# A hybrid four-layer network on one core: six edits to its order and its small operations

## The chip, the cores and the metric

The kernel runs on one core of one Trainium2 chip. The core has a matrix engine (TensorE, PE in the profile, with its weight loads shown as PEld), a vector engine (VectorE, DVE), an activation engine (ScalarE, ACT), GpSimd (POOL) and a queue engine for transfers (SyncE, SP). The time is the device time of one launch in microseconds (us); a kernel's time is the median of several runs. One more execution of the kernel was recorded by the hardware profiler; all rows below are from it.

## The reference

A sequence of 256 rows of 1024 numbers passes through two blocks of two layers each, all in float32. The projection weights are read from memory once; nothing is reused between layers.

```
def first_block(x, mem, ...):                 # the first two layers
    for l in range(DEPTH):
        mix = hybrid_mixer(h, ...)            # rnn branch + windowed attention with sinks
        h = layer_norm(ALPHA * h + mix, ...)                      # ln1
        h = layer_norm(ALPHA * h + cross_attention(h, mem, ...))  # ln2
        h = layer_norm(ALPHA * h + swiglu(h, ...))                # ln3
def rglru_branch(...):  # log_a = -8 * r * softplus(-lru_lambda), a scan over the sequence
def swa_sink_branch(...):
    probs = softmax(concatenate([scores, sink], axis=-1))[..., :-1]
def second_block(x, ...):                     # the last two layers
    for l in range(DEPTH):
        proj = rms_norm(x, pre_norm[l]) @ w_in[l]
        o = diff_attention(q, k, v, lam, rel_bias)   # w = p0 - lam * p1, then w @ v
        y_a = rms_norm(o) * (1 - lam_init) * silu(z_a)
        filt = hyena_filters(...)                    # depends on the weights alone
        z = fft_long_conv(hv, filt[:, 0]) * hx1
        z = fft_long_conv(z, filt[:, 1]) * hx2
        m = sigmoid(g_a) * (y_a @ w_pa[l]) + sigmoid(g_h) * (y_h @ w_ph[l])
        x = x + rms_norm(m @ w_out[l], post_norm[l])
```

## The kernel before

**Matrices.** Each float32 factor is split into a high part (suffix h) and a low part (suffix l), and a product takes three matmuls: high by high, high by low, low by high. A weight is loaded by SP into a tile `raw`, copied by ACT into `wh` (L240) and subtracted by DVE into `wl` (L242), in halves of 128x1024. Activations are turned by PE with transposes (L393) into a layout with features on partitions; the two parts are then taken from PSUM by ACT and DVE (`split`, L369 and L371). `fm` is a result with features on partitions, `tm` one with rows on partitions.

**Order.** PE and SP run in exactly the order in which the program issues their work. The orders on ACT, DVE and POOL are made by a scheduler at build time from priorities and an estimate of readiness. What the program issues is set by generators: one main stream walks over the weights, piece by piece, and beside it chains (`rnn_co`, the attentions, the filters) take turns. A chain hands over with `yield L["name"]`; the number in the table L (L46 to L53) says after how much estimated time it may go on. A larger number puts the next step of the chain, its PE instructions included, behind more matmuls of the main stream.

**The places of this change.** `vec_co` transposes the small vectors and computes the decay rates of the rnn branch on DVE and ACT (L580 to L592). `swa_run` does the windowed attention: scores from PSUM (L710), maximum (L714), maximum with the sink (L716), its negation (L717), exponentials (L721), transposes `pt`, row sums turned with `rb` (L746 reads them). `to_fm_block` transposes a normed block (`tx`), ahead of it a few matmuls on constants (`warm`, L529) whose count stands in `WARM`. The filters' last products `fh` are taken from PSUM by ACT into `ft` (L1354). `pre_co` does the norm ahead of the second block's projections. In `diff_attention` the weights `dsc` of two heads are transposed (`dw`), multiplied with v (`o`), normed (`yo`), transposed (`yt`) and split into `ya2h` and `ya2l`, which the next weight stream (`fm` from `ya2h`) reads. `c` is the last product of the inverse Fourier transform, from `Yh` and `Yl`.

Of the kernel before, what the change touches and what calls it, by code (L numbers as in the profile page):

```python
# [13 lines left out]
F32 = mybir.dt.float32  # L14
# [6 lines left out]
P = 128  # L21
# [25 lines left out]
    vec=6000, flt=12000, fh=1200, fe=18000, prep=15000, mlp=7500, sc=11000, rnn=7000, rnn2=11700,  # L47
    pt=3000, tx=0, spec=6000, sp0=3000, sp1=5000, sp2=5000, sp3=5000, ds=9000, dn=8960, do=5500,
    z=12000, cn=1000, cp=2000, ln_0=500, ln01=5500, ln02=5500, ln03=6800, ln_03=2300, ln11=6000, ln12=4000, pre0=5100,
    pre1=5000, rope=5000, sw0=1120, sw_end=1500, sw1=1000, sw2=1500, cv0=800, cv1=1050, rnn3=1800,  # L50
    rnn_end=3000, cx0=1500, cx1=1000, cx2=800, cx_end=1500, ml=7200, fm=3000, fm1=7500, fe0=4000, eo0=6000,
    eo1=12000, eo2=8000, fd=6000, di0=1500, dw=2300, di_end=1500, c30=770, c31=1300, hy0=1300,
    hy1=2000, hy2=500, hy3=1600, hy_end=2000, pre_n=3000, pre_b=2500, pre_n0=1000, pre_n1=2300, prep2=30000, mem=10200, mt=2500, vt=2500, vt2=12000)  # L53

# [35 lines left out]

WARM = {"ln0": 3, "ln1": 3, "pre0": (9, 0), "pre1": (9, 0), "pt": 4}

# [18 lines left out]
class Net:  # L111
    def __init__(self, ctx, tc, a):
        self.tc, self.nc, self.a = tc, tc.nc, a
        self.const = ctx.enter_context(tc.tile_pool(name="const", bufs=1))
        self.wraw = ctx.enter_context(tc.tile_pool(name="wraw", bufs=NRAW))
        self.wspl = ctx.enter_context(tc.tile_pool(name="wspl", bufs=NW))
        self.slots = ctx.enter_context(tc.tile_pool(name="slots", bufs=NSLOT))
        self.sm = ctx.enter_context(tc.tile_pool(name="sm", bufs=2))
        self.ps = ctx.enter_context(tc.tile_pool(name="ps", bufs=4, space=PSUM))
        self.pa = ctx.enter_context(tc.tile_pool(name="pa", bufs=4, space=PSUM))  # L120
        self.dr = ctx.enter_context(tc.tile_pool(name="dr", bufs=1, space=bass.MemoryType.DRAM))
        self.n = 0
        self.first_hi = None
        self.wm = None
        self.block_1 = None
        self.start = True

        self.pause, self.defer = False, None
        self.t = 0.0
        self.chains, self.bg, self.fill = [], [], True  # L130
        nc = self.nc
        self.ident = self.const.tile([P, P], F32, name="ident")
        make_identity(nc, self.ident)
        self.mhalf = self.const.tile([P, 4], F32, name="mhalf")
        nc.vector.memset(self.mhalf, -0.5)
# [356 lines left out]

    def to_fm_block(self, src, x, tb, warm=0, after=None):

        t = slice(tb * P, (tb + 1) * P)
        for q in range(2):
            ps = self.pch([4, P], "tx")
            self.busy(ps, 0 if q else warm)
            for i in range(4):
                k = q * 4 + i  # L500
                self.tr(ps[:, i, :], src[tb][:, k * P:(k + 1) * P])
            self.fm_ins = self.split(x[0][q][:, :, t], x[1][q][:, :, t], ps, after)
            if self.pause and tb == TB - 1 and q == 1:
                self.resume(self.fm_ins[1])
            yield L["tx"]
# [28 lines left out]
    def load_common(self):  # L534
# [4 lines left out]
        for nme in self.VEC1:  # L539
            if nme == "conv_w":  # L540
                cnt, s = 32, a[nme].rearrange("l k (c p) -> (k c) l p", p=P)
            else:
# [10 lines left out]
        nc.gpsimd.dma_start(self.sink, a["sinks"].rearrange("l h -> (l h)")[None, :]  # L553
                            .to_broadcast([P, DEPTH * 16]))

    def vec_co(self):
# [3 lines left out]
        for l in range(DEPTH):  # L560
# [9 lines left out]
            self.half_ig.append(hb)  # L570
            self.rates.append(self.decay_rates(l))
        if self.both:
            yield L["vt2"]
            yield from self.block2_vecs()

# [57 lines left out]
    def ln_co(self, l, i, t, hT):  # L633
# [5 lines left out]
        yield L[f"ln{l}{i}"] - first  # L639
        yield from self.to_fm_block(t, hT, 1, warm=WARM["ln1"] * self.pause)  # L640

# [45 lines left out]
    def swa_run(self, l, s, kv):  # L687
        nc = self.nc
        sink = self.sink[:, l * 16:(l + 1) * 16]
        yield L["sw1"] + L["sw2"] * kv  # L690
        for tb in (1, 0):
# [5 lines left out]
            m, ng, es, dn = (stt[:, i, :] for i in range(4))  # L697
            sk = sink[:, kv * 8:kv * 8 + 8]
            for r0 in range(0, 4, nh):
# [8 lines left out]
                for e in range(2):  # L708
# [6 lines left out]
                    scs.append(sc)  # L715
                nc.vector.tensor_tensor(m[:, hs], m[:, hs], sk[:, hs], op=ALU.max)  # L716
                nc.vector.tensor_scalar(ng[:, hs], m[:, hs], -1.0, None, op0=ALU.mult)  # L717
                for e, sc in enumerate(scs):
# [4 lines left out]
                if r0 + nh == 4:  # L723
                    nc.vector.tensor_tensor(es, sk, m, op=ALU.subtract)
                    nc.scalar.activation(es, es, AF.Exp)
# [614 lines left out]
    def filter_mul(self, l, o, hf, wos, res):  # L1340
# [4 lines left out]
        for d, w in enumerate(wos):  # L1345
            if late:
                fts.append(self.slot("ft", [TB, 512]))
            for tb in range(TB):
# [4 lines left out]
                if late:  # L1353
                    nc.scalar.activation(fts[d][:, tb, :], ps, AF.Copy)  # L1354
                    yield 0
                else:
                    nc.vector.tensor_tensor(hf[d][:, tb, :], ps, hf[d][:, tb, :], op=ALU.mult)
                    yield L["fh"]
# [281 lines left out]
    def pre_co(self, l, s):  # L1640
# [22 lines left out]
        for tb in range(TB):  # L1663
            yield (L["pre_n"] if l else L["pre_n0"]) if tb == 0 else L["pre_n1"]
            yield from self.to_fm_block(xn, s.hT, tb, WARM[f"pre{l}"][tb], vi)

# [183 lines left out]
```

## Time and profile before

| | |
|---|---|
| median of 3 runs | 1526.6 us (1525.53 to 1526.72) |
| the profiled execution | 1525.07 us, of which the span of its instructions is 1523.0 us |
| PE busy | 1500.3 us (99%) |
| DVE busy | 1095.7 us (72%) |
| ACT busy | 862.6 us (57%) |
| POOL busy | 83.0 us (5%) |

PE is busy nearly all of the span, so the time is the sum of PE's work and of the short stretches in which it waits for another engine. In a row of the timeline the first number is the start in us from the beginning of the span, the second the time until the end of the last instruction of the row, and the brackets give the idle time ahead of it and what ended it. Two matmuls in a row overlap in the records: eight matmuls on 256 columns [rows 14] start in two groups of four at 1469.16 and 1469.64, so 0.12 us apart, though each is shown as 0.28 us long. An idle time of PE in brackets is therefore shorter than what the wait costs, by some 0.16 us each.

### The profile page before, as it was taken

To read this page: it belongs to the slowest core of one execution; us is meant where nothing else is said; L and a number is where in the kernel's file an instruction comes from. 1 tells how busy PE (TensorE), PEld (TensorE's weight loads), DVE (VectorE), ACT (ScalarE), POOL (GpSimd) and SP (SyncE) were. 2 spreads that over 40 slices of the span, in tenths; PEclk is the share of its full clock that TensorE was granted. 3 is DMA by queue.
4 is the path that set the end of the run, shared out by engine and by line. 5 is a ranking of instruction groups with operands and counts; after the bars stand their busy time and mean duration, and the time that the engine had idled before them with its cause. 6 is when DMAs were issued, how large, how long until landed. Compare 5 with 4: busy or idle time off the path is not lost. (4 is left out here: it accounts for less than half of the span.)

```text
span 1523.0 us, 25811 instructions
## 1 busy us (share of the span) xinstructions
PE 1500.3 (99%) x10621; PEld 1382.1 (91%) x10625; DVE 1095.7 (72%) x1583; ACT 862.6 (57%) x1338; POOL 83.0 (5%) x153
## 2 busy tenths in 40 slices
PE   9999999999999999999999999999999999999997
PEld 7889999989999989899989889999898999898996
DVE  5966667668665577868676777555997977997965
ACT  5789444545444445797345557644645664555752
POOL 4001000000000000001010010000000000000000
PEclk9999999999999999999999999999999999999999
DMA  8434655545545555436556476575355346354442
GB/s 291 136 119 159 222 186 174 183 150 198 189 166 194 182 170 175 131 120 220 199 185 204 148 237 218 170 242 187 107 156 182 122 168 206 125 172 138 158 162 83
DMA packets 202982, 263.93 MB, mean 173 GB/s; under 512 B 5491, under 2 KB 163413, under 8 KB 202864
## 3 DMA queue, kind: packets, MB, share of 16 engines
q1 hardware_dynamic: 197232, 246.43, 48.7%
q0 software_dynamic: 5632, 15.86, 3.5%
q8 instruction: 83, 1.36, 0.4%
q14 instruction: 35, 0.29, 0.1%
HBM read 261.21 MB, written 2.11 MB: 173 GB/s over the span
## 5 line engine op out<-in xcount | busy, mean ns | idle before, releaser
L242 DVE TENSOR_TENSOR wl<-raw,wh 128x1024 fp32r<-128x1024 f32 x464 | 567.2, 1226 | 288.0 <-ACT wh L240 286.8
L240 ACT ACTIVATE wh<-raw 128x1024 fp32r<-128x1024 f32 (+1 forms) x465 | 490.2, 1057 | 447.3 <-PE fm L381 246.0
L381 PE MATMUL fm<-n2h,wh 128*128 128x256 f32 x640 | 172.2, 287 | 0.5 <-ACT n2h L369 0.5
L381 PE MATMUL fm<-n2h,wl 128*128 128x256 f32 x640 | 170.1, 283 | 0.0
L381 PE MATMUL fm<-n2l,wh 128*128 128x256 f32 x640 | 169.6, 283 | 0.0
L381 PE MATMUL fm<-h2h,wh 128*128 128x256 f32 x704 | 149.6, 284 | 1.7 <-ACT h2h L369 1.2
L381 PE MATMUL fm<-h2h,wl 128*128 128x256 f32 x704 | 149.4, 283 | 0.0
L381 PE MATMUL fm<-h2l,wh 128*128 128x256 f32 x704 | 149.0, 283 | 0.0
L381 PEld LDWEIGHTS fm<-n2h,wh 128*128 128x128 f32 x640 | 117.8, 191 | 3.4 <-issue 2.0
L381 PEld LDWEIGHTS fm<-h2h,wh 128*128 128x128 f32 x704 | 114.0, 192 | 5.0 <-issue 1.5
L381 PEld LDWEIGHTS fm<-n2h,wl 128*128 128x128 f32 x640 | 117.8, 192 | 0.1
L381 PEld LDWEIGHTS fm<-n2l,wh 128*128 128x128 f32 x640 | 117.6, 192 | 0.0
L381 PEld LDWEIGHTS fm<-h2h,wl 128*128 128x128 f32 x704 | 113.1, 192 | 0.5 <-issue 0.4
L381 PEld LDWEIGHTS fm<-h2l,wh 128*128 128x128 f32 x704 | 113.0, 192 | 0.0
L381 PE MATMUL fm<-xTh,wh 128*128 128x256 f32 x256 | 69.1, 288 | 0.0
L381 PE MATMUL ff<-wh,ah 128*128 128x512 f32 x176 | 68.9, 392 | 0.0
L381 PE MATMUL fm<-h3h,wh 128*128 128x256 f32 x256 | 68.9, 287 | 0.0
L381 PE MATMUL ff<-wl,ah 128*128 128x512 f32 x176 | 68.7, 390 | 0.0
L381 PE MATMUL ff<-wh,al 128*128 128x512 f32 x176 | 68.5, 389 | 0.0
L381 PE MATMUL fm<-h3h,wl 128*128 128x256 f32 x256 | 67.9, 283 | 0.0
L381 PE MATMUL fm<-xTh,wl 128*128 128x256 f32 x256 | 67.8, 283 | 0.0
L381 PE MATMUL fm<-h3l,wh 128*128 128x256 f32 x256 | 67.8, 283 | 0.0
(437 smaller groups left out, 3623.0 us busy)
## 6 DMA issues: line engine op xcount, KB each, us to landing
raw<-in_w_in_dram SPq DMA_DIRECT2D x89, 1024.0 KB, 5.2
raw<-in_ffn_wi_dram SPq DMA_DIRECT2D x44, 1024.0 KB, 5.1
raw<-in_ffn_wo_dram SPq DMA_DIRECT2D x22, 1024.0 KB, 4.9
raw<-in_w_out_dram SPq DMA_DIRECT2D x16, 1024.0 KB, 5.1
raw<-in_ckv_w_dram SPq DMA_DIRECT2D x16, 1024.0 KB, 5.2
raw<-in_w_br_attn_dram SPq DMA_DIRECT2D x8, 1024.0 KB, 4.9
raw<-in_w_br_rnn_dram SPq DMA_DIRECT2D x8, 1024.0 KB, 5.0
raw<-in_cq_w_dram SPq DMA_DIRECT2D x8, 1024.0 KB, 4.8
```

Of the source, the lines that this page charges most:

```text
L240: hi_ins = self.nc.scalar.activation(hi[:, i:i + q], s[:, i:i + q], AF.Copy)
L242: lo_ins = self.nc.vector.tensor_tensor(lo, s, hi.bitcast(F32), op=ALU.subtract)
L381: self.nc.tensor.matmul(out, lhsT=l, rhs=r, start=start, stop=stop)
```

## The change

Six edits stand in it. The decay rates of layer 1 are computed after a further pause of `vec_co`. In the windowed attention a new constant `nsink`, the negated sinks, is made once, and one operation takes minus the maximum and the minimum with `nsink`, where two operations took the maximum with the sink and its negation. One matmul on constants stands ahead of the attention's `pt` where four stood. The splits of the second row block of the norms `ln2` are held behind the last filter eviction `ft` on their engine. The second row block of the second block's first norm waits 1500 in the table where it waited 2300. The transposes `dw` wait 10300 where they waited 8960.

```diff
-    pt=3000, tx=0, ..., ds=9000, dn=8960, do=5500,
+    pt=3000, tx=0, ..., ds=9000, dn=10300, do=5500,
-    hy1=2000, ..., pre_n0=1000, pre_n1=2300, prep2=30000, ...
+    hy1=2000, ..., pre_n0=1000, pre_n1=2300, pre_n2=1500, prep2=30000, ...
-WARM = {"ln0": 3, "ln1": 3, "pre0": (9, 0), "pre1": (9, 0), "pt": 4}
+WARM = {"ln0": 3, "ln1": 3, "pre0": (9, 0), "pre1": (9, 0), "pt": 1}
...
-            self.fm_ins = self.split(x[0][q][:, :, t], x[1][q][:, :, t], ps, after)
+            with self.tc.issue_after(behind.ins) if behind else nullcontext():
+                self.fm_ins = self.split(x[0][q][:, :, t], x[1][q][:, :, t], ps, after)
...
-            self.rates.append(self.decay_rates(l))
+            if l == 0:
+                nc.vector.tensor_scalar(self.nsink, self.sink, -1.0, None, op0=ALU.mult)
+            if l == 0:
+                self.rates.append(self.decay_rates(l))
         if self.both:
             yield L["vt2"]
+        self.rates.append(self.decay_rates(1))
+        if self.both:
             yield from self.block2_vecs()
...
-        yield from self.to_fm_block(t, hT, 1, warm=WARM["ln1"] * self.pause)
+        yield from self.to_fm_block(t, hT, 1, WARM["ln1"] * self.pause,
+                                    behind=self.ft_ins if self.pause else None)
...
-                nc.vector.tensor_tensor(m[:, hs], m[:, hs], sk[:, hs], op=ALU.max)
-                nc.vector.tensor_scalar(ng[:, hs], m[:, hs], -1.0, None, op0=ALU.mult)
+                nc.vector.scalar_tensor_tensor(ng[:, hs], m[:, hs], -1.0, nsk[:, hs],
+                                               op0=ALU.mult, op1=ALU.min)
...
-                    nc.vector.tensor_tensor(es, sk, m, op=ALU.subtract)
+                    nc.vector.tensor_tensor(es, sk, ng, op=ALU.add)
...
-                    nc.scalar.activation(fts[d][:, tb, :], ps, AF.Copy)
+                    self.ft_ins = nc.scalar.activation(fts[d][:, tb, :], ps, AF.Copy)
...
-            yield (L["pre_n"] if l else L["pre_n0"]) if tb == 0 else L["pre_n1"]
+            yield (L["pre_n"] if l else L["pre_n0"]) if tb == 0 else (
+                L["pre_n1"] if l else L["pre_n2"])
```

The order of instructions moves at many places. The first is the beginning of DVE's queue, where the weights' low parts are made; `wl_180` before and `wl_181` in the change are the same half of the second weight load, `sink` is the constant that POOL loads. Before:

```order
L371 TENSOR_TENSOR xTl_91<-tx_197,xTh_89 128x4x128
L371 TENSOR_TENSOR xTl_92<-tx_204,xTh_90 128x4x128
L242 TENSOR_TENSOR wl_180<-raw_127,wh_179 128x1024
L242 TENSOR_TENSOR wl_184<-raw_127,wh_183 128x1024
L242 TENSOR_TENSOR wl_218<-raw_129,wh_217 128x1024
```

The same place in the change:

```order
L371 TENSOR_TENSOR xTl_91<-tx_198,xTh_89 128x4x128
L371 TENSOR_TENSOR xTl_92<-tx_205,xTh_90 128x4x128
L574 TENSOR_SCALAR nsink<-sink 128x32
L242 TENSOR_TENSOR wl_181<-raw_127,wh_180 128x1024
L242 TENSOR_TENSOR wl_185<-raw_127,wh_184 128x1024
L242 TENSOR_TENSOR wl_219<-raw_129,wh_218 128x1024
```

The operation that makes `nsink` stands ahead of the low part `wl_181`, and every low part stands behind it.

The second place is on PE in the first layer of the second block, where the transposes `dw` of the first row block's second pair of heads stand; `fm_...` are matmuls of the main stream, in groups of 24. Before:

```order
L381 MATMUL fm_12613<-n2l_11238,wh_12523 128x256
L393 MATMUL dw_12700<-ident,dsc_12405 128x128 x4
L381 MATMUL fm_12707<-n2h_11235,wh_12554 128x256
...
L381 MATMUL fm_12707<-n2l_11238,wh_12554 128x256
L381 MATMUL c_1839_12737<-Yh_12558,dft_9089 128x512
L381 MATMUL c_1839_12737<-Yl_12559,dft_9089 128x512
L381 MATMUL c_1839_12737<-Yh_12558,dft_9089 128x512
L381 MATMUL c_1839_12737<-Yh_12642,dft_9089 128x512
L381 MATMUL c_1839_12737<-Yl_12643,dft_9089 128x512
```

In the change:

```order
L381 MATMUL fm_12678<-n2l_11225,wh_12532 128x256
L381 MATMUL c_1834_12708<-Yh_12536,dft_9076 128x512
L381 MATMUL c_1834_12708<-Yl_12537,dft_9076 128x512
L381 MATMUL c_1834_12708<-Yh_12536,dft_9076 128x512
L381 MATMUL c_1834_12708<-Yh_12613,dft_9076 128x512
L381 MATMUL c_1834_12708<-Yl_12614,dft_9076 128x512
...
L381 MATMUL c_1835_12716<-Yh_12613,dft_9076 128x512
L393 MATMUL dw_12724<-ident,dsc_12383 128x128 x4
L381 MATMUL fm_12678<-n2h_11222,wh_12578 128x256
```

The twelve matmuls `c` stand ahead of the transposes `dw`, and the 24 matmuls of the main stream that stood between them are gone from there.

The third place is on PE in the last layer, where the last transposes `yt` of the attention stand ahead of the stream that reads `ya2h`. Before:

```order
L381 MATMUL fm_15554<-n2l_13662,wh_15423 128x256
L393 MATMUL yt_15583<-ident,yo_15502 128x128 x4
L381 MATMUL fm_15554<-n2h_13659,wh_15458 128x256
...
L381 MATMUL fm_15554<-n2l_13662,wh_15458 128x256
L381 MATMUL fm_15621<-ya2h_14734,wh_15519 128x256 x4
L381 MATMUL fm_15621<-ya2h_14734,wl_15520 128x256 x4
L381 MATMUL fm_15621<-ya2l_14735,wh_15519 128x256 x4
```

In the change:

```order
L381 MATMUL fm_15541<-n2h_13671,wl_15440 128x256
L381 MATMUL fm_15541<-n2l_13673,wh_15439 128x256
L393 MATMUL yt_15601<-ident,yo_15536 128x128 x4
L381 MATMUL fm_15608<-ya2h_14721,wh_15470 128x256 x4
L381 MATMUL fm_15608<-ya2h_14721,wl_15471 128x256 x4
L381 MATMUL fm_15608<-ya2l_14722,wh_15470 128x256 x4
```

The 24 matmuls that stood between the transposes and the first reader of their split now stand ahead of the transposes.

## Rows read from the trace of the kernel before

**Rows 1.** Waits of PE: who waited for whom, total us, times, longest.

```profile
PE qt L393 <- DVE kv L671: 1.5, 1, 1.5
```

**Rows 2.** Timeline of DVE at the rates of layer 1.

```profile
48.40 0.17 DVE L590 TENSOR_TENSOR rates<-rates 128x8 f32<-128x8 f32 x1 [1.35 <-ACT rates L588]
```

**Rows 3.** Timeline of DVE, 11 to 18 us.

```profile
13.57 2.36 DVE L242 TENSOR_TENSOR wl<-raw,wh 128x1024 fp32r<-128x1024 f32 x2 [1.44 <-ACT wh L240]
```

**Rows 4.** Instructions of the tile sink, and its transfer.

```profile
L553 POOL DMA_DIRECT2D sink<-in_sinks_dram x1: 549/549/549, 11.7 to 11.7; - x1
...
DMA to landing us min/median/max: 5.3/5.3/5.3
```

**Rows 5.** Timeline of PE, 15 to 16.2 us.

```profile
15.58 0.39 PE L381 MATMUL tm<-wl,xTh 128*128 128x512 f32 x1
```

**Rows 6.** Timeline of DVE in layer 1's windowed attention.

```profile
637.01 0.16 DVE L717 TENSOR_SCALAR sst<-sst 128x4 f32<-128x4 f32 x1
```

**Rows 7.** Timeline of PE there.

```profile
637.86 1.91 PE L393 MATMUL pt<-ident,scs 128*128 128x128 f32 x8 [1.30 <-ACT scs L721]
...
644.75 0.66 PE L393 MATMUL rb<-ident,rbs 128*128 128x128 f32 x4
```

**Rows 8.** Timeline of ACT there.

```profile
643.45 0.65 ACT L746 ACTIVATE rbs<-rb 128x512 f32<-128x512 f32 x1
644.12 1.28 ACT L841 ACT_TABLE_LOAD   x1
645.41 1.06 ACT L841 ACTIVATE gr<-gr 128x1024 f32<-128x1024 f32 x1
```

**Rows 9.** Timeline of PE at ln2 of layer 1.

```profile
876.34 0.82 PE L529 MATMUL tx<-wm 128*128 128x512 bf16 x3
...
879.58 0.73 PE L381 MATMUL fm<-h2h,wh 128*128 128x256 f32 x4 [0.51 <-ACT ft L1354]
881.54 0.73 PE L381 MATMUL fm<-h2h,wh 128*128 128x256 f32 x4 [1.23 <-ACT h2h L369]
```

**Rows 10.** Timeline of ACT there.

```profile
878.94 2.06 ACT L1354 ACTIVATE ft<-fh 128x512 f32<-128x512 f32 x4
880.85 0.65 ACT L369 ACTIVATE h2h<-tx 128x512 fp32r<-128x512 f32 x1
```

**Rows 11.** Timeline of PE at the second block's first norm.

```profile
1085.70 1.23 PE L381 MATMUL fm<-n2h,wh 128*128 128x256 f32 x8 [0.47 <-ACT n2h L369]
```

**Rows 12.** Timeline of PE at the transposes dw, third layer.

```profile
1203.46 0.41 PE L393 MATMUL dw<-ident,dsc 128*128 128x128 f32 x2 [0.26 <-DVE dsc L1520]
1204.37 0.44 PE L393 MATMUL dw<-ident,dsc 128*128 128x128 f32 x2 [0.50 <-DVE dsc L1520]
```

**Rows 13.** Timeline of DVE there.

```profile
1207.18 1.28 DVE L371 TENSOR_TENSOR Yl<-t,Yh 128x512 fp32r<-128x512 f32 x2
```

**Rows 14.** Timeline of PE ahead of the last layer's stream from ya2h.

```profile
1466.21 0.36 PE L381 MATMUL fm<-n2h,wh 128*128 128x256 f32 x1
...
1469.16 0.64 PE L381 MATMUL fm<-ya2h,wh 128*128 128x256 f32 x4
1469.64 0.64 PE L381 MATMUL fm<-ya2h,wl 128*128 128x256 f32 x4
```

**Rows 15.** Timeline of DVE there.

```profile
1468.29 0.68 DVE L371 TENSOR_TENSOR ya2l<-yt,ya2h 128x512 fp32r<-128x512 f32 x1
```

**Rows 16.** Timeline of PE at the same place of the third layer.

```profile
1246.02 0.60 PE L393 MATMUL yt<-ident,yo 128*128 128x128 f32 x4
```

**Rows 17.** Timeline of DVE there.

```profile
1249.70 0.69 DVE L371 TENSOR_TENSOR ya2l<-yt,ya2h 128x512 fp32r<-128x512 f32 x1
```

**Rows 18.** Timeline of PE, 5.4 to 8 us.

```profile
5.53 1.85 PE L529 MATMUL warm<-wm 128*128 128x512 bf16 x4
```

**Rows 19.** Windows: PE, PEld, DVE, ACT, POOL busy (instructions), granted clock, DMA share, GB/s.

```profile
1514.00:1519.00 5.00, 0.15 (x1) 0.00 (x0) 2.63 (x5) 0.69 (x2) 0.56 (x1) 1.00 0.56 210
1519.00:1523.00 4.00, 0.00 (x0) 0.00 (x0) 0.00 (x0) 0.00 (x0) 0.00 (x0) 0.53 0.00 0
```

More of the change, by code (lines that the diff above doesn't have):

```diff
@@ L47 @@
     vec=6000, flt=12000, fh=1200, fe=18000, prep=15000, mlp=7500, sc=11000, rnn=7000, rnn2=11700,
-    pt=3000, tx=0, spec=6000, sp0=3000, sp1=5000, sp2=5000, sp3=5000, ds=9000, dn=8960, do=5500,
+    pt=3000, tx=0, spec=6000, sp0=3000, sp1=5000, sp2=5000, sp3=5000, ds=9000, dn=10300, do=5500,
     z=12000, cn=1000, cp=2000, ln_0=500, ln01=5500, ln02=5500, ln03=6800, ln_03=2300, ln11=6000, ln12=4000, pre0=5100,
@@ L52 @@
     eo1=12000, eo2=8000, fd=6000, di0=1500, dw=2300, di_end=1500, c30=770, c31=1300, hy0=1300,
-    hy1=2000, hy2=500, hy3=1600, hy_end=2000, pre_n=3000, pre_b=2500, pre_n0=1000, pre_n1=2300, prep2=30000, mem=10200, mt=2500, vt=2500, vt2=12000)
+    hy1=2000, hy2=500, hy3=1600, hy_end=2000, pre_n=3000, pre_b=2500, pre_n0=1000, pre_n1=2300, pre_n2=1500, prep2=30000, mem=10200, mt=2500, vt=2500, vt2=12000)
 def shape_constants():
@@ L126, in __init__ @@
         self.start = True
-        self.pause, self.defer = False, None
+        self.pause, self.defer, self.ft_ins = False, None, None
         self.t = 0.0
@@ L491, in rstd, with to_fm_block @@
         self.nc.gpsimd.tensor_tensor(out, out, self.mhalf[:, :n], op=ALU.pow)
-    def to_fm_block(self, src, x, tb, warm=0, after=None):
+    def to_fm_block(self, src, x, tb, warm=0, after=None, behind=None):
         t = slice(tb * P, (tb + 1) * P)
@@ L554, in load_common @@
                             .to_broadcast([P, DEPTH * 16]))
+        self.nsink = self.const.tile([P, DEPTH * 16], F32, name="nsink")
     def vec_co(self):
@@ L688, in swa_run @@
         nc = self.nc
-        sink = self.sink[:, l * 16:(l + 1) * 16]
+        sink, nsink = (x[:, l * 16:(l + 1) * 16] for x in (self.sink, self.nsink))
         yield L["sw1"] + L["sw2"] * kv
@@ L697, in swa_run @@
             m, ng, es, dn = (stt[:, i, :] for i in range(4))
-            sk = sink[:, kv * 8:kv * 8 + 8]
+            sk, nsk = (x[:, kv * 8:kv * 8 + 8] for x in (sink, nsink))
             for r0 in range(0, 4, nh):
```

## The prediction, made before the changed kernel ran

> **What bounds the kernel now.** I read the waits of PE first. Their list shows few entries, and the three that this change names are a group of transposes `qt` that waits once for 1.5 us on DVE [rows 1], the transposes `pt` [rows 7] and the transposes `dw` [rows 12]. PE runs in program order, so what a PE wait costs is not regained later: the next matmuls simply start later. I then read, for each of the six edits, the order of the changed kernel on PE, ACT and DVE, and set beside each changed place the timelines of the three engines. The question at each place is which engine delivers last. PE's spacing is the third thing to read: matmuls of 256 columns start 0.12 us apart, so the first eight that read `ya2h` keep PE busy for 0.96 us [rows 14]; matmuls on constants take 0.216 us each, from (0.82 - 0.16)/3 with 0.16 for the overhang of the last one [rows 9].
>
> **Later decay rates: nothing.** The wait of `qt` comes from DVE, which waits 1.35 us for ACT's logarithm in the rates of layer 1 and only then copies `kv` for the transposes [rows 1, 2]. The edit puts a pause ahead of these rates. In the changed order, however, they stand at the same places of ACT and DVE, ahead of that copy, because the scheduler of these engines places them by readiness. I take 0; were the rates really late, -1.5 would be the other end.
>
> **One operation for maximum and negation.** Twelve groups lose an operation of 0.16 us on DVE [rows 6]; the time counts only where DVE releases PE, which is at `pt` of layer 1, below. What the edit adds is one operation that makes `nsink`, and its place decides. It stands on DVE's queue directly ahead of the low part of the third half weight, which before starts at 13.57 [rows 3], and it needs the transferred sinks. POOL issues that transfer at 11.7 and it lands 5.3 us later, at 17.0 [rows 4]. Until then DVE stands still, and behind the small operation are queued every low part of the weights. So `wl` starts at about 17.1 and, at 1.2 us each (2.36 for two that overlap), ends at 18.35. The matmul that reads it started at 15.58 [rows 5]; it now starts at about 18.4. That is +2.8 us. Nothing later in the first 60 us has slack against a fixed time that would give it back: loads of weights are issued as buffers come free and so shift with it. Bounds: 0, if the transfer lands before 13.6; +4, if PE then also stays behind the low parts one by one for some halves.
>
> The Trainium skill (DMA: Bandwidth & Descriptors, Anatomy of one DMA) gives a transfer issued by GpSimd a fixed cost of about 2.0 us plus its bytes. By that, an estimate from this page, the sinks would land at about 13.8, DVE would lose 0.2 us and PE nothing. The row shows 5.3 us, so the sum goes by the row; what the page would make of it is one of the rivals.
>
> **One matmul on constants in place of four.** They stand right ahead of the `pt` that waits 1.30 us for ACT's exponentials [rows 7], so the three that go (0.65 us) would by themselves only lengthen that wait. The scheduler has also moved DVE's work: ahead of these exponentials it now has one split `xcl` fewer and the operation of 0.16 us fewer, and the weight half that stood ahead of the scores is moved behind them, so the exponentials come early enough and the wait goes: -1.30 - 0.16 (the overhang) - 0.65 = -2.1. What is late next stands in ACT's order. Before, ACT took `rbs` from PSUM at 643.45 and only then loaded a table (1.28 us) and did `gr` (1.06 us) [rows 8], and PE's next `rb` came at 644.75, just 0.65 us after the end of `rbs` [rows 7]. Now table and `gr` stand ahead of `rbs`. It is late by up to 2.3 us, less the 0.65 of slack: about +1.6. I take -0.5, with -2.1 and +0.5 as ends.
>
> The Trainium skill (ScalarE: Activation LUTs, What ACT_TABLE_LOAD costs) adds a drain of about 1.38 us to each table load of 1.28 us. With it the new wait would be 3.0 and the sum 1.4 us higher. In the trace `rbs` ends at 644.10, the load starts at 644.12, and the next activation starts 1.29 us later [rows 8], so there is no room for it.
>
> **Splits behind the filter evictions.** At ln2 PE waits 0.51 for an eviction `ft`, does four matmuls and waits 1.23 for the split `h2h`, which stood behind four `ft` of 2.06 us together [rows 9, 10]. In the changed order the `ft` come first and the splits follow directly, so PE has one wait in place of two, and the matmuls after it start together. Before, the place after four matmuls was reached at 881.54. Now the transposes end near 879.0, two splits of some 0.5 to 0.6 us follow, PE starts at about 880.25 and reaches that place at 880.7: -0.8. Ends: 0 and -1.5.
>
> **The first norm of the second block.** Earlier transposes and fewer filter products between them let ACT do the splits `n2h` ahead of two `ft`, so the wait of 0.47 [rows 11] goes. The first matmul there needs a PSUM buffer which the `ft` free, and these now stand behind two more splits, some 1.1 us. The four filter products that left this place are done later and cost the same there. I take +0.3, with -0.6 and +1.2 as ends.
>
> **Later transposes `dw`.** Before, PE waits 0.26 and 0.50 for `dsc` [rows 12], with the overhang 1.1 us per layer. This goes in both layers. But `c` now stands where `dw` and 24 matmuls stood, 24 x 0.12 = 2.9 us and four transposes earlier. Its fifth matmul needs the second pair of low parts `Yl`, which DVE starts at 1207.18 and of which the first ends at 1207.86 [rows 13]. Without its waits and the 24 matmuls PE would get there at about 1206.6, 1.2 us too early, and more if DVE is held by a weight half. So one wait is exchanged for another: +0.2 per layer, ends -1.1 and +0.9.
>
> The same number moves the whole chain behind it. In the last layer the final `yt` now has no matmul at all between itself and the first that reads its split; before, 24 matmuls (from 1466.21 to 1469.16) stood there [rows 14]. If the splits come as before, `ya2l` ends at 1468.97 [rows 15]. PE, which is free at 1466.21, would reach its first reader 0.96 us later at 1467.17. That is a wait of 1.8, most of it ahead of `ya2h`. In the third layer two products of 512 columns (about 0.46) stand between: `yt` is through at 1246.02 + 0.36 = 1246.38 [rows 16], `ya2l` would be reached at 1247.8 and is ready at 1250.39 [rows 17]: +2.6. The 24 matmuls themselves stay; only the cover is gone. Ends of both together: +1.2 (a split of 0.6 right behind the transposes) and +6.
>
> **Sum.** 0 + 2.8 - 0.5 - 0.8 + 0.3 + 0.4 + 1.8 + 2.6 = +6.6. The profiled execution took 1525.07, so 1531.7; the median of the runs is 1.5 above it, so 1533.2, and I say 1533.
>
> **Rivals.** *The cover is not needed.* The later `dw` spares its waits (-2.2 for both layers) and DVE, no longer hurried by them, has `Yl` and the last splits done when PE arrives; then 2.8 - 0.5 - 0.8 + 0.3 - 2.2 gives -0.4, 1526.2, no slower than before. For it: DVE has idle time in the stretch of the last splits. Against it: `yt`, split and reader depend on each other, and in the last layer nothing stands between them. It decides at the point where `ya2l` ends within 0.96 us of `yt`. *The sinks land early,* before 13.6: 2.8 goes, 1530.4. Against it stands the row of 5.3 us [rows 4]; for it, the figure of the Trainium skill quoted above. *The clock falls at the new idle time of 2.8 us.* The longest wait inside the full-speed stretch before was 1.5 [rows 1]. The first matmuls on constants ran at half speed, 0.42 us each (from 1.85/4 with the overhang) against 0.216 [rows 18, 9]; a few us of that would cost 2 to 3 more, 1536. Against it: after the last matmul at 1514 the granted clock still reads 1.00, the level of 2.4 GHz, up to 1519, with almost no work on PE [rows 19]. *The rates are really late* and `qt` stops waiting: 1531.7.
>
> **Chances.** The forecast 0.62, its own range 1530.5 to 1536.5; the cover not needed 0.14; sinks early 0.10; the clock 0.07; the rates 0.07. A measurement of this kernel tells a change from none at about 0.2%, 3 us, so from 1529.7 it is slower. The forecast, the clock and most of the two between lie above that: slower 0.82. No slower: same 0.14, faster 0.04, for the case in which the cover isn't needed and the start costs little as well. The range that leaves two in ten out is 1528 to 1538.
>
> **What would show it.** Right: an idle time of PE near 15.6 us of 2.5 to 3 us, ended by `wl`, and of DVE ended by the transfer of the sinks; waits of PE for `ya2h` and `ya2l` ahead of both streams, 1.5 to 2.7 in all at each; `c` waiting for `Yl` in place of `dw` for `dsc`; `rb` waiting for `rbs` in layer 1; the wait of `qt` unchanged. Wrong: no DVE idle time ahead of the third low part, or no wait at the two streams, or a granted clock below 1.00 after 18 us.

## The result, and the profile after

The changed kernel took 1534.14 us (median of 4 runs, 1534.01 to 1534.89), the kernel before 1526.34 us beside it (4 runs, 1525.53 to 1526.72). The ratio is 1.0052, with a 95% interval of 1.0040 to 1.0064: 7.8 us slower. The forecast said 1533: 6.6 us on top of the profiled execution of before, and 1.5 because the median of its runs lies above that execution. The profiled execution of the changed kernel took 1534.14, its span 1532.4.

The busy times, from the page of the changed kernel:

```profile
PE 1500.6 (98%) x10619; PEld 1383.0 (90%) x10622; DVE 1094.8 (71%) x1572; ACT 866.6 (57%) x1342; POOL 82.8 (5%) x153
```

PE is as busy as before (1500.6 against 1500.3 us), so most of what was added is time in which PE waits. Its waits in the changed kernel (who waited for whom: us in total, times, longest):

```profile
PE tm L381 <- DVE wl L242: 3.1, 2, 2.8
PE fm L381 <- ACT ya2h L369: 2.9, 2, 1.7
PE c L381 <- DVE Yl L371: 2.3, 2, 1.2
PE tm L381 <- ACT wh L240: 1.8, 1, 1.8
PE fm L381 <- ACT ft L1362: 1.7, 1, 1.7
PE rb L393 <- ACT rbs L754: 1.7, 1, 1.7
PE qt L393 <- DVE kv L679: 1.5, 1, 1.5
```

In the kernel before, PE did not wait for `ya2h` or `Yl`, and waited at most 0.3 for `wl`, 0.5 for `ft` and 0.4 for `rbs`. `qt` waits as it did [rows 1]. The wait for `wh` ends when the first weight is there, and that time differs from execution to execution: in the thirteen profiles of this document the first matmul that reads a weight starts between 6.92 and 8.68 us, though PE, ACT and DVE do the same things in the same order up to there in all of them.

Where the time came from is read by setting the start of the same PE instruction of the two profiled executions side by side, all along the program. Each number is taken where PE has done the same work in both; behind the first norm of the second block, four filter products `fh` that the changed kernel does later (4 x 0.23 = 0.9 us) are added.

| up to and with | changed minus before, us | step | forecast |
|---|---|---|---|
| first matmul of the first weight | 0.5 | +0.5 | 0 |
| low part of the third half weight (15.58, now 19.07) | 3.5 | +3.0 | +2.8 |
| rnn, layer 0, to the attention of layer 1 | 3.6 | +0.1 | 0 |
| attention of layer 1 | 2.7 | -0.9 | -0.5 |
| rnn, layer 1 | 3.3 | +0.6 | 0 |
| ln2 of layer 1 | 2.55 | -0.75 | -0.8 |
| first norm of the second block | 3.75 | +1.2 | +0.3 |
| `c` and `dw`, third layer | 4.3 | +0.6 | +0.2 |
| stream from `ya2h`, third layer | 7.6 | +3.3 | +2.6 |
| norm of the last layer | 6.4 | -1.2 | 0 |
| `c` and `dw`, last layer | 7.0 | +0.6 | +0.2 |
| stream from `ya2h`, last layer | 9.4 | +2.4 | +1.8 |

The 9.4 belongs to these two executions, the 7.8 to the medians: the profiled execution of before lay 1.3 under the median of its runs.

**The start.** The changed kernel's timelines of DVE and PE, and the transfer of the sinks with its time from issue to landing:

```profile
17.70 0.18 DVE L574 TENSOR_SCALAR nsink<-sink 128x32 f32<-128x32 f32 x1 [5.11 <-DMA sink<-in_sinks_dram]
17.79 3.49 DVE L242 TENSOR_TENSOR wl<-raw,wh 128x1024 fp32r<-128x1024 f32 x3
```

```profile
19.07 0.50 PE L381 MATMUL tm<-wl,xTh 128*128 128x512 f32 x1 [2.83 <-DVE wl L242]
```

```profile
L554 POOL DMA_DIRECT2D sink<-in_sinks_dram x1: 542/542/542, 12.2 to 12.2; - x1
...
DMA to landing us min/median/max: 5.5/5.5/5.5
```

DVE stands still for 5.11 us for 0.18 us of work (1.44 us of it stood there before too, for `wh` [rows 3]), and three low parts of weights come behind it without a gap. PE's matmul of [rows 5] waits 2.83 for the first of them. Issue at 12.2 and 5.5 us make 17.7; the row of before [rows 4] had said 5.3.

**Attention of layer 1.** The matmuls on constants of the kernel before, then PE and ACT of the changed kernel:

```profile
614.58 1.04 PE L529 MATMUL pt<-wm 128*128 128x512 bf16 x3
```

```profile
647.31 0.66 PE L393 MATMUL rb<-ident,rbs 128*128 128x128 f32 x4 [1.70 <-ACT rbs L754]
...
651.00 0.39 PE L381 MATMUL fm<-h3h,wh 128*128 128x256 f32 x1
```

```profile
644.42 1.28 ACT L849 ACT_TABLE_LOAD   x1
645.72 1.06 ACT L849 ACTIVATE gr<-gr 128x1024 f32<-128x1024 f32 x1
646.68 0.58 ACT L754 ACTIVATE rbs<-rb 128x512 f32<-128x512 f32 x1
```

The wait of `pt` is gone, and `rb` has 1.70 in its place, since the table load and `gr` now stand ahead of `rbs` where they stood behind it [rows 8]. The matmuls on constants (four; the trace holds three of them) do not stand ahead of the `pt` that waited at 637.86: they start at 614.58, ahead of the attention's first `pt`, for which PE did not wait. Three fewer of them save 0.65 there.

**The streams from ya2h.** In the third layer, PE, then ACT, then windows (PE, PEld, DVE, ACT, POOL busy, granted clock, DMA share, GB/s):

```profile
1252.78 0.60 PE L393 MATMUL yt<-ident,yo 128*128 128x128 f32 x4
1253.13 0.70 PE L381 MATMUL fh<-fwo,a 128*128 128x512 f32 x2
1255.09 0.74 PE L381 MATMUL fm<-ya2h,wh 128*128 128x256 f32 x4 [1.25 <-ACT ya2h L369]
...
1256.58 1.01 PE L381 MATMUL fm<-ya2l,wh 128*128 128x256 f32 x4 [0.28 <-DVE ya2l L371]
1257.39 0.41 PE L381 MATMUL fm<-ya2h,wh 128*128 128x256 f32 x1
...
1260.16 0.33 PE L381 MATMUL fm<-ya2h,wl 128*128 128x256 f32 x1
```

```profile
1252.52 0.60 ACT L866 ACTIVATE sb<-fm 128x512 f32<-128x512 f32 x1 [1.82 <-PE fm L381]
1253.01 1.05 ACT L240 ACTIVATE wh<-raw 128x1024 fp32r<-128x1024 f32 x1
1253.96 0.59 ACT L1362 ACTIVATE ft<-fh 128x512 f32<-128x512 f32 x1
1254.44 0.60 ACT L369 ACTIVATE ya2h<-yt 128x512 fp32r<-128x512 f32 x1
```

```profile
1255.00:1256.00 1.00, 0.91 (x7) 0.92 (x8) 1.00 (x2) 1.00 (x4) 0.00 (x0) 1.00 0.00 0
1258.00:1259.00 1.00, 1.00 (x7) 1.00 (x6) 0.86 (x2) 0.00 (x0) 0.00 (x0) 0.50 1.06 412
```

Two things are seen here. `yt` was through near 1253.1, but ACT first finished `sb`, half a weight and an eviction `ft`, and came to `ya2h` at 1254.44: the wait of 1.25. And after it the matmuls start 0.21 us apart instead of 0.12, while the granted clock reads 0.50, the level of 1.2 GHz; from 1256.58 to 1260.16 that is 17 matmuls in 3.58 us instead of 17 x 0.12 = 2.04, so 1.5 us. In the last layer, PE and ACT, and below them ACT at the same place of the kernel before (there `yt` starts at 1465.85):

```profile
1475.78 0.60 PE L393 MATMUL yt<-ident,yo 128*128 128x128 f32 x4
1478.06 0.74 PE L381 MATMUL fm<-ya2h,wh 128*128 128x256 f32 x4 [1.68 <-ACT ya2h L369]
...
1479.43 0.74 PE L381 MATMUL fm<-ya2l,wh 128*128 128x256 f32 x4 [0.16 <-DVE ya2l L371]
```

```profile
1475.98 0.60 ACT L866 ACTIVATE sb<-fm 128x512 f32<-128x512 f32 x1 [1.82 <-PE fm L381]
1476.47 1.05 ACT L240 ACTIVATE wh<-raw 128x1024 fp32r<-128x1024 f32 x1
1477.42 0.59 ACT L369 ACTIVATE ya2h<-yt 128x512 fp32r<-128x512 f32 x1
```

```profile
1466.05 1.06 ACT L240 ACTIVATE wh<-raw 128x1024 fp32r<-128x1024 f32 x1 [1.34 <-PE fm L381]
1467.02 0.58 ACT L369 ACTIVATE ya2h<-yt 128x512 fp32r<-128x512 f32 x1
```

Nothing stands between `yt` and its reader. ACT did half a weight ahead of `ya2h` before too; what is new ahead of it is the eviction `sb`, so that `ya2h` starts 1.64 us behind the start of `yt` instead of 1.17. Here the clock stayed at 1.00.

**The norm of the last layer.** PE's second group of transposes `tx`, before and in the changed kernel:

```profile
1301.35 1.32 PE L393 MATMUL tx<-ident,xn 128*128 128x128 f32 x8 [0.89 <-DVE xn L1657]
```

```profile
1310.65 1.04 PE L393 MATMUL tx<-ident,xn 128*128 128x128 f32 x8
```

Twelve matmuls `fd` of the filters now stand between the two groups, and the wait of 0.89 is gone. The same step of -1.2 is in the profile of the later `dw` alone (below), so it comes with that edit.

### The profile page after: what moved, and what is told of

It is laid out like the page before. It is cut to its first block, busy times and chain, and to the rows that moved or that the text cites. A ratio compares the mean times of both kernels' runs of the same rounds, so it can differ in the third digit from the quotient of the medians.

```text
span 1532.4 us, 25785 instructions
## 1 busy us (share of the span) xinstructions
PE 1500.6 (98%) x10619; PEld 1383.0 (90%) x10622; DVE 1094.8 (71%) x1572; ACT 866.6 (57%) x1342; POOL 82.8 (5%) x153
```

## The experiments

Every kernel was timed beside the kernel before; a ratio is to that, with its 95% interval. In a diff, a line with - is of the kernel that the heading names as its base, and ... stands for what is left out.

**The later dw alone** (base: before).

```diff
-    ..., dn=8960, do=5500,
+    ..., dn=10300, do=5500,
```

> The kernel before with the later transposes dw alone (dn 10300 for 8960). Cover theory: the two streams that read ya2h lose the matmuls that stood between the last yt and their first reader, so PE waits there for ya2h and ya2l, some 1.5 and 1.8 us, and c waits for Yl in place of dw for dsc: 5 us slower than before, 1531.5, of which 0.3 per layer from c. Rival: the waits at the two streams in the changed kernel come from the rest of the change, which makes ACT and DVE late in the second block; then dn alone spares the waits of dw and is 2 us faster, 1524.5.

Measured: 1533.23 us (1530.63 to 1537.74, 6 runs) against 1525.87, ratio 1.0049 (1.0035 to 1.0064). One number of the table does nearly all of what the six edits did together. Its waits of PE, and windows in both streams:

```profile
PE fm L381 <- ACT ya2h L369: 3.4, 2, 1.7
PE c L381 <- DVE Yl L371: 2.3, 2, 1.2
PE fm L381 <- DVE ya2l L371: 1.5, 2, 1.4
```

```profile
1253.00:1255.00 2.00, 0.76 (x3) 0.77 (x4) 2.00 (x4) 0.17 (x1) 0.00 (x0) 0.50 0.06 18
...
1479.00:1481.00 2.00, 2.00 (x11) 2.00 (x11) 0.00 (x0) 0.00 (x0) 0.00 (x0) 0.50 0.92 343
```

The cover was needed, and the rival that `dw` would spare time falls. The price is 7.4 us where the terms for `c` and the two streams said 4.8; here both streams ran partly at half clock, which the terms did not hold. In the trace `c` and `dw` cost 0.6 in each layer and the streams 5.7 and 3.8, and the norm of the last layer gives 1.2 back. Its single times go with the mean granted clock of their execution: 1530.63 at 0.998, 1532.35 at 0.997, 1534.12 at 0.995, 1537.74 at 0.992.

**The one operation with nsink alone** (base: before).

```diff
+            if l == 0:
+                nc.vector.tensor_scalar(self.nsink, self.sink, -1.0, None, op0=ALU.mult)
...
-                nc.vector.tensor_tensor(m[:, hs], m[:, hs], sk[:, hs], op=ALU.max)
-                nc.vector.tensor_scalar(ng[:, hs], m[:, hs], -1.0, None, op0=ALU.mult)
+                nc.vector.scalar_tensor_tensor(ng[:, hs], m[:, hs], -1.0, nsk[:, hs],
+                                               op0=ALU.mult, op1=ALU.min)
...
```

> The kernel before with the one operation for maximum and negation alone. Queue theory: the operation that makes nsink stands ahead of the third low part and waits for the sinks, so PE idles 2.8 us near 16 to 19 us and the kernel is 2.5 to 3 us slower, 1529.2. Rival: the idle time at the start comes from weights that landed later in that execution (the first weights were waited for 1.8 us there); then there is no new wait, twelve operations fewer cost nothing, and the time is that of before, 1526.3.

Measured: 1529.43 us (1527.56 to 1531.01, 11 runs) against 1525.87, ratio 1.0021 (1.0012 to 1.0029), so 3.6 us. PE waits 2.81 for `wl` at 19.50, and in this execution the clock fell right behind that wait:

```profile
20.00:22.00 2.00, 2.00 (x6) 1.52 (x5) 2.00 (x3) 0.00 (x0) 2.00 (x4) 0.50 0.12 11
```

In the profile of the full change the same wait, of 2.83, was followed by a clock of 1.00. At the attention of layer 1 the wait of `pt` is gone in this kernel too, with four matmuls on constants still there, and `rb` waits 0.94 in its place: it is this edit that takes the wait of `pt` away. Whether the operation saved or the new order on DVE does it, no run takes apart.

That 3.6 lies so near the expected 2.5 to 3 is partly luck. In the trace the wait costs 3.0, the attention of layer 1 gives 1.4 back, which the expectation did not count, and the clock takes 1.7 behind the wait and 1.5 more at `ln2`, where it reads 0.50 from 886.5 to 889.9 behind a wait of 1.22 that the kernel before has too [rows 9].

**The changed kernel with nsink made later** (base: changed).

```diff
-            nc.vector.tensor_scalar(hb, self.vec1(l, "b_ig"), 0.5, None, op0=ALU.mult)
+            hbi = nc.vector.tensor_scalar(hb, self.vec1(l, "b_ig"), 0.5, None, op0=ALU.mult)
...
-                nc.vector.tensor_scalar(self.nsink, self.sink, -1.0, None, op0=ALU.mult)
+                with self.tc.issue_after(hbi.ins):
+                    nc.vector.tensor_scalar(self.nsink, self.sink, -1.0, None, op0=ALU.mult)
```

> The whole change, with the operation that makes nsink held behind a later small operation on the vector engine (near 51 us). Queue theory: the idle time at 16 to 19 us goes, 3 us faster than the change, 1531.2; the waits at the two streams stay. Rival (weights landed later): no difference from the change, 1534.

Measured: 1531.21 us (1530.87 to 1532.85, 5 runs), ratio 1.0034 (1.0022 to 1.0046). DVE now makes `nsink` at 41.9, where nothing waits for it, and PE's wait is gone. The kernel is 5.3 above before, where the full change was 7.8 above: 2.5 us less, of 3.0 seen in the trace. The two intervals overlap a little, but the wait is gone from the trace, so most of that edit's price is its place in the queue and not the operation. The streams from `ya2h` wait as in the changed kernel (2.9 in two) and ran at a clock of 1.00 in this execution. But at the attention of layer 1, behind the same wait of 1.70 as in the changed kernel, the clock fell:

```profile
644.29 0.66 PE L393 MATMUL rb<-ident,rbs 128*128 128x128 f32 x4 [1.70 <-ACT rbs L755]
645.01 3.34 PE L381 MATMUL y<-pt,kv 128*64 128x512 f32 x8
648.29 1.40 PE L381 MATMUL sc<-kv,qT 64*128 64x128 f32 x16
649.62 0.39 PE L381 MATMUL fm<-h3h,wh 128*128 128x256 f32 x1
```

```profile
645.00:648.00 3.00, 2.99 (x8) 0.72 (x8) 2.34 (x4) 1.11 (x2) 0.00 (x0) 0.57 0.41 138
```

From `rb` to the first `fm` it takes 5.33 us (649.62 - 644.29); in the changed kernel the same 28 instructions took 3.69 (651.00 - 647.31). That is the price of one such fall: 1.6 us. All six profiles with the changed attention and one matmul on constants have this wait of 1.70, and the clock fell at it in four: here, with the cover back, in the four other edits and in the last version below.

**Cover back in front of the streams** (base: the one with nsink later).

```diff
-    ..., dn=10300, do=5500,
+    ..., dn=10300, do=3500,
```

> As e3_nsink_late, and the step from the attention's product to the transposes yt shortened (do 3500 for 5500), so that the last yt stand one group of 24 matmuls earlier again while dw stay where the change puts them. Cover theory: the waits for ya2h and ya2l ahead of both streams go, some 3.5 to 4 us faster than e3_nsink_late, about 1527.5; the wait of c for Yl stays. Rival: the splits are late because ACT and DVE are late in the whole of that stretch; then the waits stay and the time is that of e3_nsink_late.

Measured: 1527.17 us (1525.97 to 1528.80, 11 runs), ratio 1.0007 (0.9999 to 1.0016). The waits for `ya2h` and `ya2l` are gone, and 4.0 us with them. `c` still waits 2.3 for `Yl`, since `dw` is still late.

**The four other edits** (changed kernel, nsink later, dw where it was).

```diff
-    ..., dn=10300, do=5500,
+    ..., dn=8960, do=5500,
```

> The change without its two costly parts: nsink held behind a later small operation, dw back at 8960; rates, splits behind the filter evictions, one matmul ahead of pt and the earlier norm transposes stay. By the terms of the prediction -0.5, -0.8 and +0.3: 1 us faster than the kernel before, about 1525; e3 less the price of the later dw (7.4 us as e1 has it) would give 1524. Rival: the small gains are not there, and the time is 1526 or more.

Measured: 1525.76 us (1523.84 to 1527.12, 11 runs) against 1526.25, ratio 0.9997 (0.9988 to 1.0005). What is left of the change is -0.5 us, not to be told from nothing; the terms said -1.0.

**The rates really late** (base: the four other edits).

```diff
-        self.rates.append(self.decay_rates(1))
+        with self.tc.issue_after(self.kt_ins.ins):
+            self.rates.append(self.decay_rates(1))
...
-        nc.vector.tensor_copy(s.kT, ps)
+        self.kt_ins = nc.vector.tensor_copy(s.kT, ps)
```

> As e5_four_left, and the decay rates of layer 1 are really held behind the copy of the keys for which PE waits 1.5 us near 50 us. Theory (DVE stands behind ACT's logarithm at that place): the wait goes, 1.5 to 1.8 us faster than e5_four_left. Rival: DVE's copy is late for another reason, such as the eviction before it, and less than 0.5 us is gained.

Measured: 1524.50 us (1521.79 to 1526.03, 11 runs), ratio 0.9988 (0.9979 to 0.9996). Held behind the copy, the rates let `qt` start without a wait, as its row without a bracket shows:

```profile
48.66 1.91 PE L393 MATMUL qt<-ident,q 128*128 128x128 f32 x16
```

The medians are 1.3 us apart, near the 1.5 of [rows 1], but the two intervals overlap; in the two traces the way from 23 to 67 us differs by 1.6. The pause of the change did not make the rates late; this does.

**Matmuls on constants in the gap behind yt** (base: the later dw alone).

```diff
+        if tb:
+            self.busy(self.pst([512], "warm"), 6)
```

> As e1_dn_alone, with six matmuls on constants behind the last yt of each layer, 1.3 us that lie inside the waits for ya2h. Clock theory: what e1_dn_alone lost beyond its waits, and the spread of its single times (1530.6 to 1537.7), comes from the granted clock that falls to half after these waits in some executions; with PE busy there it stays at 1.00, the median is 1530.8, near the lowest time of e1_dn_alone, and the times lie within 1.5 us. Rival: the spread has another source (transfers), and the median stays near 1533 or rises by the added matmuls.

Measured: 1531.03 us (1530.21 to 1531.77, 6 runs) against 1526.25, ratio 1.0033 (1.0021 to 1.0046). With more work on PE it is 4.8 above before, where the later `dw` alone was 7.4 above. The two intervals overlap, so the 2.6 us between them is not sure by itself; the runs, though, lie within 1.6 us instead of 7.1. Its third layer, PE and a window:

```profile
1250.58 1.46 PE L529 MATMUL warm<-wm 128*128 128x512 bf16 x6
1252.43 0.74 PE L381 MATMUL fm<-ya2h,wh 128*128 128x256 f32 x4 [0.39 <-ACT ya2h L369]
```

```profile
1255.00:1257.00 2.00, 2.00 (x16) 2.00 (x17) 2.00 (x4) 0.00 (x0) 0.00 (x0) 1.00 0.64 189
```

The constants fill time in which PE would have waited, and the clock stays at 1.00 where it read 0.50 with the later `dw` alone. The mean clock of its six executions averages 0.9977, that of the later `dw` alone 0.9953. This, the smaller spread and the medians together make it likely that a part of the price of the later `dw` is the clock and not the waits. That the constants are what keeps the clock up is not shown by single profiles: with nsink later the clock stayed at 1.00 in both streams without them. In this execution it fell elsewhere, from 638.6 to 642.0, behind the wait of 1.29 for `pt`, where the kernel before had 1.00 behind 1.30 [rows 7].

**The splits behind the evictions alone** (base: before).

```diff
-            self.fm_ins = self.split(x[0][q][:, :, t], x[1][q][:, :, t], ps, after)
+            with self.tc.issue_after(behind.ins) if behind else nullcontext():
+                self.fm_ins = self.split(x[0][q][:, :, t], x[1][q][:, :, t], ps, after)
...
```

> The kernel before with the splits of ln2 held behind the filter evictions alone. By the prediction's term -0.8 us, 1525.4: one wait of PE of about 1.2 us for h2h in place of 0.51 and 1.23. Rival: the later splits are also read later, and the time is 1526.2 as before.

Measured: 1525.14 us (1524.42 to 1527.66, 11 runs) against 1526.30, ratio 0.9995 (0.9985 to 1.0004). The two waits of [rows 9] became one of 1.17, as forecast; the time can't be told from no change, though the medians point the right way. In this execution the clock was 0.50 from 881 to 884, behind that wait. All but one of the single times fall into two groups by the clock: seven of 1524.4 to 1525.2 at a mean clock of 0.998 or 0.999, three of 1527.3 to 1527.7 at 0.996.

**One matmul on constants alone** (base: before).

```diff
-WARM = {..., "pt": 4}
+WARM = {..., "pt": 1}
```

> The kernel before with one matmul on constants ahead of pt in place of four, alone. Theory of the prediction, that these matmuls lie inside the wait: the wait of 1.30 us for the exponentials grows by 0.65, and the time is 1526.2 within 0.4. In the change this wait went by the operation saved on DVE and by the new order of DVE; alone it should stay. Rival: this edit by itself gives the gain of some 0.5 us at this place.

Measured: 1526.09 us (1525.52 to 1528.85, 11 runs), ratio 1.0000 (0.9991 to 1.0008). The wait grew by 0.99, from the 1.30 of [rows 7], where the expectation had 0.65:

```profile
638.32 2.16 PE L393 MATMUL pt<-ident,scs 128*128 128x128 f32 x8 [2.29 <-ACT scs L721]
```

PE is 0.65 us earlier behind the attention's first `pt`, where the constants stand, and waits that out here, 22 us later. So the fewer constants lengthen the wait, as the working had it, though from another place; what takes it away is the one operation with `nsink` (above). The clock fell at this wait as well, to 0.50 from 638.2 to 641.6.

**The earlier second row block of the first norm alone** (base: before).

```diff
-    ..., pre_n1=2300, prep2=30000, ...
+    ..., pre_n1=2300, pre_n2=1500, prep2=30000, ...
...
-            yield (L["pre_n"] if l else L["pre_n0"]) if tb == 0 else L["pre_n1"]
+            yield (L["pre_n"] if l else L["pre_n0"]) if tb == 0 else (
+                L["pre_n1"] if l else L["pre_n2"])
```

> The kernel before with the earlier transposes of the second block's first norm alone (1500 for 2300). By the prediction's term +0.3 us, 1526.5: the wait of 0.47 us for n2h goes, and one of some 1.7 us for the filter evictions comes, ahead of which stand fewer filter products. Rival: the change of order of ACT there gives a gain, 1525.5 or less.

Measured: 1526.75 us (1525.97 to 1527.44, 11 runs), ratio 1.0002 (0.9994 to 1.0011). The wait for `ft` came (1.7 at its longest); the price, +0.45 in the medians, is too small to be told from nothing. The trace has +1.2 at this norm and -0.8 at the norm of the last layer, where the four moved filter products now stand and the wait for `xn` is 0.34 instead of 0.89.

**A version from what was learnt** (base: the rates really late; the first norm as before, dw at 9500).

```diff
-    ..., dn=8960, do=5500,
+    ..., dn=9500, do=5500,
...
-            yield (L["pre_n"] if l else L["pre_n0"]) if tb == 0 else (
-                L["pre_n1"] if l else L["pre_n2"])
+            yield (L["pre_n"] if l else L["pre_n0"]) if tb == 0 else L["pre_n1"]
```

> A version built from what the runs showed: as e6_rates_late, without the earlier norm transposes (the wait behind the evictions there cost more than it gave), and dw at 9500, between the two values. By the terms: e6_rates_late less 0.3 to 1.5 us, 1521.5 to 1523, faster than the kernel before. Rival: at 9500 the last yt already stand too close to their readers, and the time is 1525 or more.

Measured: 1521.77 us (1520.62 to 1523.86, 8 runs) against 1526.25, ratio 0.9972 (0.9962 to 0.9982): 4.5 us faster than before, where the changed kernel was 7.8 slower. Its waits of PE:

```profile
PE rb L393 <- ACT rbs L756: 1.7, 1, 1.7
...
PE c L381 <- DVE Yl L371: 0.9, 2, 0.5
```

At 9500 `dw` no longer waits for `dsc`, `c` waits 0.9 in place of 2.3, and no wait for `ya2h` or `ya2l` is left. Between 8960 and 10300 there is a place where `dw` is late enough for its weights and the splits of `yt` still have their cover. In the trace the steps for `c` and `dw` are worth only 0.4 in each layer; more, 1.2, comes at the norm of the last layer, where the twelve `fd` now stand between the two groups of `tx` as in the changed kernel. The terms by which 1521.5 to 1523 was expected did not hold that.

## Why the prediction was right, and where its sizes were off

*The time and the sign.* 1534.14 lies 1.1 above the forecast of 1533 and inside its own range. The mechanism at the start (term +2.8, measured 3.0 in the trace and 2.5 by taking it away) held to the detail: a 0.18 us operation at the head of an in-order queue, waiting for a transfer. So did that of the lost cover: the later `dw` alone loses it, and the shorter `do` brings it back. That the total is so near is partly luck: of the 9.4 in the traces, 0.5 is the first weight's arrival and 1.5 the clock, a gain of 1.2 was not seen, and several terms were off by 0.4 to 0.9. Of the signs named, all five of the right ones came, and one of the wrong ones, the clock.

*Rates: 0.* The wait of `qt` was unchanged at 1.5. The rival of late rates was wrong for this change, but right on what they would bring.

*Attention: -0.5.* The trace gave -0.9: PE gained 2.95 up to the end of `pt` where the term had 2.1, and lost 2.05 at `rb` where it had 1.6. One reading was wrong. The matmuls on constants do not stand right ahead of the `pt` that waits but 22 us earlier, at 614.58. The sum took no harm, since a gain there is waited out at 637.86 as long as PE waits there. At this place the runs separate the edits: `nsink` alone takes the wait of `pt` away, and fewer constants alone lengthen it to 2.29.

*ln2 and the first norm: -0.8 and +0.3.* The traces gave -0.75 and +1.2, with the waits named (one wait of 1.17 at ln2; 1.72 for `ft` at the norm). At the norm the wait of 1.72 in place of 0.47 is the whole +1.2, the upper end of the term. Its time alone, +0.45, agrees with the term only because the moved filter products fill a later wait, which the term did not hold. In time only the sum of the four other edits could be looked at, and -0.5 with an interval of about 1.3 us on both sides fits without showing any one.

The Trainium skill (ScalarE: Activation LUTs, What ACT_TABLE_LOAD costs) has a drain of about 1.38 us beside a table load. Here the load starts at 644.42 and the next activation at 645.72, 1.30 later, and the wait behind it was 1.70 and not the 3.0 that was estimated with the drain.

*The later dw: +0.2 for each layer, +1.8 and +2.6 for the streams.* For `c` and `dw` the steps were +0.6 in each layer: the wait for `Yl` of 1.17, with the slower starts around it, costs 1.7 where the term had 1.3. For the last layer 2.4 came instead of 1.8: the term assumed that the splits come as they did before, but the eviction `sb` now stands ahead of them on ACT and makes them 0.5 later. For the third layer 3.3 came instead of 2.6, and for another reason than given. The wait was for `ya2h` on ACT, 1.25, and not for `ya2l` on DVE, and it was shorter than the term; 1.5 us of the 3.3 are the clock. The gain of 1.2 at the norm of the last layer was in no term.

*The clock.* The text called a granted clock below 1.00 after 18 us a sign that it is wrong, and it did read 0.50 around 1258. As a rival the clock had 0.07 and stood at the start alone, weighed by the end of the program, where it stayed up for 5 us with almost no work [rows 19]. That row was the wrong neighbour: it told how long an idle PE keeps its clock once, and the falls came behind waits of 1.2 to 2.8 us with matmuls around them. The same instructions took 1.6 us longer behind `rb` when it fell, so it is a cost of its own beside the waits.

*Not forecast:* a wait of 0.44 for `rbs` in layer 0's attention went (-0.5), and waits of 0.29 for `wl` came at 159.72 and at 709.72, one ahead of the attention of layer 1 and one behind it (+0.55 each). All three are in the profile of the one operation with nsink alone, and in none of those that leave this operation out. The two for `wl` stay when nsink is made later, so they do not come from the stall at the start; why the new order makes them is open.

Open too is the sum of the parts: alone they give +7.4, +3.6, -1.2, -0.2 and +0.45, together 10 where the whole gave 7.8. The clock is a likely cause and not shown to be it: the six executions of the later `dw` alone have a mean clock of 0.9953, the four of the changed kernel 0.997, and 0.0017 of 1530 us is 2.6 us, an estimate.

## What to carry to other kernels

Where an engine works in order, a new small operation costs what stands behind it while its input is on the way: look up when the input lands before placing it, and hold it behind something later. A matmul chain that waits for its own result through PSUM and a split needs other matmuls between; a number that moves the chain's start also moves its end, so look at both. Where short waits lie close together, count a fall of the clock as well as the wait, and try whether matmuls on constants in the gap pay for themselves. And compare two traces only where the engine has done the same work in both: moved instructions pass for gains and losses.

## What the runs showed of the hardware that was not expected

The granted clock falls to 0.50 behind waits of PE that are far shorter than the idle time at the end of the program, and the same instructions behind the same wait do not always get it. The wait of 1.70 at `rb` was followed by 1.00 in the changed kernel and by 0.50 with nsink later. A wait of 2.8 at the start was followed by 1.00 in the one and by 0.50 with nsink alone. The wait of 1.3 at `pt`, which five profiles have, was followed by 0.50 in one of them. The profile of before shows no such stretch between 20 and 1514 us, but other executions of that kernel point to some: of the 75 timed beside the experiments, the 24 with a mean clock of 0.999 have a median of 1525.7 us, the 15 with 0.996 or 0.997 one of 1528.0. A fall cost 1.6 us at `rb` and 1.5 in the third layer's stream, and in the run with the later `dw` alone, where the mean clock goes from 0.998 to 0.992, times spread by 7.1 us.
